# MoBA's q reaches its transposed layout by VectorE and DRAM in place of TensorE, and its scores are taken one weight chunk later

## The chip, the core and the metric

The kernel runs on one core of a Trainium2 chip. The metric is the device time of one execution in microseconds; the time before is the median of three runs, 388.99 us (388.95 to 389.02). One further execution was profiled: it took 388.81 us, and the span from its first to its last recorded instruction is 387.0 us.

## What is computed

Two layers of a decoder trunk, 256 tokens, model width 1024, all in float32. Each layer normalises x, multiplies it by one wide matrix (1024 x 5120), and splits the result into ten column groups of 512; three attention-like branches use them, and their gated outputs are multiplied by a second matrix (1536 x 1024) and added to x. Cut to what matters here:

```python
h = rms_norm(x, norm_g[l])
proj = h @ w_in[l]
q_a, k_a, v_a, q_h, f_h, i_h, q_m, z = jnp.split(proj, split_points, axis=-1)
qa = partial_rope(rms_norm(q_a.reshape(B, S, 8, 64), moba_q_norm[l]), positions)
ka = partial_rope(rms_norm(k_a.reshape(B, S, 8, 64), moba_k_norm[l]), positions)
o_a = moba_attention(qa, ka, va)                # 256 tokens are one block: causal softmax(qa ka^T / 8) va
o_h = hgrn2_chunkwise(q_h, f_h, i_h, lb_all[l]) # gated linear recurrence, 4 heads of 128
o_m = memory_attention(qm, km, vm)              # softmax over 256 memory tokens, 4 heads of 128
y = jnp.concatenate([o_a, o_h, o_m], axis=-1) * jax.nn.silu(z)
x = x + y @ w_out[l]
```

The change lies between q_a and the scores of `moba_attention`. With 256 tokens there is one block per head, so MoBA is plain causal attention over 8 heads of 64.

## The kernel before

**Weights.** All weights stream from DRAM in 120 chunks of 128 x 1024 (512 KB), 60 in each layer: 8 for the memory's keys and values, 40 for `w_in` (ten groups of 4), 12 for `w_out`. SyncE's queue loads a chunk into one of four buffers `wr`. ScalarE rounds it to the matmul's input type (`wh`, line 214), VectorE takes the rest (`wl = wr - wh`, line 228), and TensorE multiplies by high and low parts separately, three products for each. There are three buffers each of `wh` and `wl`; ScalarE and VectorE so work two to three chunks ahead of TensorE, and everything else that they do stands in their queues between these steps. Chunks are named below by their number in the layer: 16 to 19 are MoBA's k, 20 to 23 HGRN's input, 24 to 27 MoBA's q, 28 to 31 a gate (`zh`), 32 to 35 the memory's q (`qm`), 36 to 39 MoBA's v, 40 to 47 the two other gates, 48 to 59 `w_out`. In `group_b` (chunks 16 to 39) a chunk is 12 matmuls of 128 x 512, a group 48, and the accumulator of the first 128 tokens is complete three matmuls before the group's end.

**Order.** Branch work is written as Python generators. `slot()` and `step()` advance them between the matmuls of the chunks, and `yield n` lets n such steps pass. A scheduler then lays the instructions of each engine into one fixed order; the engines follow it without reordering and wait for each other by semaphores. `in_turn(...)` forces an order on one engine by hand (it adds no wait), `mm_row` keeps a matmul where the program has it. `order_of_attention` holds these hand-written lists for chunks 36 to 43: VectorE's and ScalarE's steps of the MoBA softmax between the weight steps.

**MoBA's q and k.** `g_qk` (line 976) takes a group's two accumulators `acc[t]`, t the half of the tokens. For each it squares and sums (lines 625, 626), takes the power -1/2 on GpSimd (`rqa`, line 982) and applies the rotary step on VectorE into `kr` (lines 985 to 992). The scores need q and k with the head dimension on the partitions. For k, `across` (line 88) does that: one VectorE transpose within 32 x 32 blocks (line 95), one DMA to DRAM (`there`, line 106), four DMAs back (line 111) into "strips", an order of columns that `strips()` describes. For q, eight TensorE transposes of 128 x 128 in two groups of four (line 1017) write PSUM, and two ScalarE copies (line 1018) make `qT`. q's norm is not applied to q but inside the softmax, as the factors `rq` and `nr` (lines 996, 998).

**Scores and softmax.** `g_moba` starts after chunk 32. The scores (lines 1113 and 1041, `sd<-kT,qT` and `acc<-kT,qT`) stand in one block of 16 matmuls; each float32 one shows as two records. VectorE masks them and takes row maxima (line 1033), `nba` (line 1056) is the negated maximum, ScalarE takes the exponentials (line 1062), VectorE divides (line 1070) and turns the probabilities by `across` through GpSimd's queue (`turned0`, `turned1`). HGRN's result `zh` and the memory branch's probabilities go through the same queue after them.

Of the kernel before, what the change touches and what calls it, by code (L numbers as in the profile page):

```python
# [28 lines left out]
EPS = 1e-6  # L29
# [16 lines left out]
def hymba_kernel(ctx: ExitStack, tc: tile.TileContext, x, mem, mem_t, positions, w_in, w_out, w_mem_kv,  # L46
# [38 lines left out]
        return sb.tile([128, n], F32, name=name, tag=name, bufs=2)  # L85


    def across(dst, src, n, stage=None, free=None, name=None, q=None, behind=None):
        q = q or nc.sync
        if stage is None:  # L90
            yield from room("blk")
            held["blk"] += 1
        tag = stage or "blk"
        blk = sb.tile([128, 4, n * 32], F32, name="blk", tag=tag, bufs=1)
        N["across", name] = nc.vector.transpose(blk.rearrange("p c (n i) -> p c n i", n=n),
                                                src.rearrange("p (n c i) -> p c n i", n=n, c=4))
        if free is not None:
            rel(free)
        if name is not None:
            done.add(name)  # L100
        yield 2
        while behind is not None and behind not in done:
            yield
        there = away.tile([4, 32, 4, n * 32], F32, name="there", tag="there", bufs=5)
        with tc.issue_after(T[behind].ins) if behind is not None else nullcontext():
            q.dma_start(there.rearrange("q j c r -> (q j) c r"), blk)
        if stage is None:
            rel("blk")
        yield 4
        for c in (0, 2, 1, 3):  # L110
            ins = q.dma_start(dst[c * 32:c * 32 + 32], there[:, :, c].rearrange("q j r -> j q r"))
# [163 lines left out]
    def mm(o, a, b, s, e):  # L275
        nc.tensor.matmul(o, lhsT=a, rhs=b, start=s, stop=e)  # L276


    def mm_row(o, a, b, s=True, e=True):
        tc.keep_in_program_order(nc.tensor.matmul(o, lhsT=a, rhs=b, start=s, stop=e))  # L280

    def group_b(th, tl):
        acc = [acc_tile() for _ in range(2)]
        for c in range(4):
            i = st["c"]
            for j in range(2):
                k = 2 * c + j
                wH, wL = whs[i][:, j * 512:(j + 1) * 512], wls[i][:, j * 512:(j + 1) * 512]
                for t in range(2):
                    ts = slice(t * 128, (t + 1) * 128)  # L290
                    mm(acc[t], th[:, k, ts], wH, k == 0, False)
# [511 lines left out]
    def g_hgrn(l):  # L803
# [8 lines left out]
        def carry(m, Tm, src, dst=None):  # L812
            (Qv, Kv), (Qo, Ko) = ([halves(a, m) for a in p] for p in (src, dst or src))
            n = 1024 // (2 * m)
            Tv = Tm.rearrange("p (n two) -> p n two", two=2)
            nc.vector.tensor_tensor(Qo[:, :, 1], Qv[:, :, 1], Tv[:, :, 0:1].to_broadcast([128, n, m]), op=OP.mult)
            nc.vector.tensor_tensor(Ko[:, :, 0], Kv[:, :, 0], Tv[:, :, 1:2].to_broadcast([128, n, m]), op=OP.mult)
# [103 lines left out]
        carry(64, T2, other)  # L921
        S2 = St.rearrange("p (a b) s -> p a b s", b=2)
        for q in range(0, 128, 32):
            nc.scalar.copy(St[q:q + 32, :, q:q + 32], hSd[q:q + 32])
        for m, o in ((32, 0), (64, 128)):
            for q in range(0, 128, 2 * m):
                for b in range(2):
                    p = q + b * m
                    nc.scalar.copy(S2[q:q + m, :, b, q + m:q + 2 * m],
                                   g[p:p + m, o:o + 4 * m].rearrange("p (a s) -> p a s", s=m))  # L930
        rel()
        Q4, K4 = (a.rearrange("p (h s) -> p h s", h=4) for a in other)
        yield 3
# [7 lines left out]
        nc.scalar.copy(xc, g)  # L941
        rel()
        yield 2
        while not {f"ih{l}", f"z{H_}{l}"} <= done:
            yield
        ih = T["ih"]
        po = []
# [25 lines left out]
    def g_qk(l, q, acc):  # L973
        ss = small("ssa", 16)
        ms = small("msa", 16)
        r = small("rka" if q else "rqa", 16)
        kr = sb.tile([128, 2, 512], F32, name="kr", tag="qk", bufs=1)
        for t in range(2):
            t8 = slice(t * 8, t * 8 + 8)
            sumsq(ss[:, t8], acc[t], 8)  # L980
            nc.vector.tensor_scalar(ms[:, t8], ss[:, t8], 1.0 / 64, EPS, op0=OP.mult, op1=OP.add)  # L981
            nc.gpsimd.tensor_tensor(r[:, t8], ms[:, t8], pw[:, :8], op=OP.pow)  # L982
            a3 = heads(acc[t], 8)
            k3 = heads(kr[:, t], 8)
            nc.vector.tensor_tensor(k3, a3, rtA[:, l, q, t][:, None, :].to_broadcast([128, 8, 64]), op=OP.mult)
# [6 lines left out]
            nc.vector.tensor_tensor(k3[:, :, 0:16], k3[:, :, 0:16], tm, op=OP.add)  # L992
            yield
        if q == 0:
            rq = small("rq", 16)
            nc.gpsimd.tensor_scalar(rq, r, 0.125, None, op0=OP.mult)
            nr = small("nr", 16)
            nc.gpsimd.tensor_scalar(nr, r, -0.125, None, op0=OP.mult)
# [8 lines left out]
        yield 2  # L1007
        tg = ("qT", "kT")[q]
        flat = kr.rearrange("p t s -> p (t s)")
        o = sb.tile([128, 1024], F32, name=tg, tag=(f"yl{M_}", f"yh{M_}")[q], bufs=1)  # L1010
        if q == 0:
            o = o.rearrange("p (h s) -> p h s", h=4)
            for t in range(2):
                yield from room("sd")
                pt = side_tile()
                for p in range(4):
                    nc.tensor.transpose(pt[:, p * 128:(p + 1) * 128], kr[:, t, p * 128:(p + 1) * 128], ident)  # L1017
                nc.scalar.copy(o[:, :, t * 128:(t + 1) * 128], heads(pt, 4))
                rel()
                yield  # L1020
# [16 lines left out]
    def second(u, ps):  # L1037
        qT, kT = T["qT"], T["kT"]
        for pi in range(2):
            for e in range(2):  # L1040
                mm_row(ps[e][:, pi * 256:(pi + 1) * 256].rearrange("p (t q i) -> p t q i", t=2, q=4),
                       qT[64 * e:64 * e + 64, 2 * u + pi, 128:256], strips(kT)[64 * e:64 * e + 64, 2 * u + pi])
        return ps

# [49 lines left out]
    def g_moba(l):  # L1094
# [20 lines left out]
        seconds = [second(0, first), second(1, [acc_tile() for _ in range(2)])]  # L1115
        yield
        for u in range(2):
            for p in (2 * u, 2 * u + 1):
# [127 lines left out]
    def order_of_attention(l):  # L1246
        c = 60 * l
        w = lambda k, i: (k, c + i)
        in_turn(("last mask", 0), ("nba", 0), ("first mask", 1), ("last mask", 1), ("nba", 1), w("wl", 36), ("ria", 0),
                *(("scale", 0, i) for i in range(5)), ("ss", "h", 0), *(("scale", 0, i) for i in range(5, 8)),  # L1250
                ("ss", "h", 1), w("wl", 37), ("across", f"turned0{l}"), ("ms", "hg"), ("ss", "qm", 0), w("wl", 38),
# [161 lines left out]
```

## Time and profile before

| | |
|---|---|
| median of three runs | 388.99 us |
| profiled execution | 388.81 us, span 387.0 us |
| granted TensorE clock | 1.000 |
| DMA, mean over the span | 218 GB/s |
| DMA, share of 16 engines: SyncE's queue, GpSimd's queue | 55.8%, 10.9% |

A row of the timeline or the chain is: start in us from the span's start, duration in us, engine (PE is TensorE, PEld its weight loads, DVE VectorE, ACT ScalarE, POOL GpSimd), source line, operation, out<-in, shape, count, and in brackets the engine's idle time before it with what ended it. Rows of one engine overlap a little, since an instruction's record runs on while the next has started. A row of a tile gives the minimum, median and maximum duration in ns. A DMA row on POOL shows the time of the issue; the landing is told apart.

### The profile page before, as it was taken

The page shows a single profiled execution, that of the slowest core. Times are in us where ns is not written, and L with a number is a line of the kernel's source. Part 1 is how long each engine was busy: PE and PEld are TensorE (multiplying, and loading weights), DVE is VectorE, ACT ScalarE, POOL GpSimd, SP SyncE. Part 2 cuts the span into 40 slices and gives each one's busy share as a digit, 9 for nine tenths or more (in the row PEclk, how much of TensorE's full clock was granted, in tenths as well). Part 3 has the DMA queues.
Part 4 walks back from the last instruction along what each step waited for, and adds up shares of the span by engine and source line. Part 5 has one row for each costly group of instructions (what it writes and reads, how often), then busy time and mean ns, then how long its engine had stood idle before and what let it go on. Part 6 is the DMA issues. An engine that isn't in the chain of part 4 may idle for free.

```text
span 387.0 us, 6782 instructions
## 1 busy us (share of the span) xinstructions
PE 381.9 (99%) x2455; PEld 319.7 (83%) x2455; DVE 320.4 (83%) x621; ACT 248.0 (64%) x414; POOL 86.8 (22%) x129
## 2 busy tenths in 40 slices
PE   8999999999999999999999999999999999999996
PEld 5888887788888888788888888888888888887885
DVE  4789799999669999967577689899698699798663
ACT  5998755567769749754375756445765985785540
POOL 3004400734203523400000040014062063232000
PEclk9999999999999999999999999999999999999999
DMA  8986594539635889985454568735766189999502
GB/s 260 420 313 202 175 329 166 164 112 285 209 105 188 269 257 341 322 255 178 161 204 164 174 208 237 252 110 179 255 190 197 54 275 271 346 300 272 188 36 108
DMA packets 26241, 84.48 MB, mean 218 GB/s; under 512 B 3552, under 2 KB 5984, under 8 KB 26208
## 3 DMA queue, kind: packets, MB, share of 16 engines
q1 hardware_dynamic: 22304, 71.31, 55.8%
q0 software_dynamic: 3616, 12.59, 10.9%
q8 instruction: 19, 0.31, 0.3%
q10 hardware_dynamic: 288, 0.15, 0.1%
q14 instruction: 14, 0.11, 0.1%
HBM read 74.60 MB, written 9.44 MB: 217 GB/s over the span
## 4 chain that ended last, share of the span: by engine, by line
PE 86%; DVE 6%; POOL 2%; issue 2%; DMA 2%; ACT 1%; SPq 0%; DVEq 0%; ACTq 0%
PE acc L276 58%; PE acc L1285 17%; PE sd L276 6%; PE sd L280 3%; DVE wl L228 2%; DMA wr<-in_w_mem_kv_dram 2%; POOL mk L605 1%; PE sd L489 1%; DVE as L360 0%; PE sd L1145 0%; PE sd L1017 0%; PE acc L280 0%; POOL rk L651 0%; DVE ssa L626 0%; DVE rt L547 0%
## 5 line engine op out<-in xcount | busy, mean ns | idle before, releaser
L214 ACT CAST wh<-wr 128x1024 fp32r<-128x1024 f32 x96 | 100.8, 1051 | 62.2 <-PE acc L276 43.1
L228 DVE TENSOR_TENSOR wl<-wr,wh 128x1024 fp32r<-128x1024 f32 x96 | 117.3, 1223 | 25.7 <-ACT wh L214 23.6
L276 PE MATMUL acc<-wh,hT 128*128 128x512 f32 x384 | 123.1, 394 | 0.1
L276 PEld LDWEIGHTS acc<-wh,hT 128*128 128x128 f32 x384 | 71.5, 188 | 15.2 <-issue 0.7
L276 PE MATMUL acc<-wl,hT 128*128 128x512 f32 x192 | 75.6, 394 | 0.0
L276 PE MATMUL acc<-hT,wh 128*128 128x512 f32 x256 | 64.0, 392 | 0.0
L276 PEld LDWEIGHTS acc<-hT,wh 128*128 128x128 f32 x256 | 46.4, 189 | 8.9 <-ACT kn L639 0.4
L276 PEld LDWEIGHTS acc<-wl,hT 128*128 128x128 f32 x192 | 36.1, 188 | 7.3
L1285 PE MATMUL acc<-wh,yl 128*128 128x512 f32 (+1 forms) x96 | 37.2, 387 | 0.0
L1285 PE MATMUL acc<-wl,yh 128*128 128x512 f32 (+1 forms) x96 | 37.2, 387 | 0.0
L232 DVE SCALAR_TENSOR_TENSOR wl<-wr,gT,wh 128x1024 fp32r<-128x1024 f32 (+1 forms) x29 | 31.2, 1098 | 6.7 <-ACT wh L218 6.6
L276 PEld LDWEIGHTS acc<-hT,wl 128*128 128x128 f32 x256 | 34.8, 190 | 2.2
L218 ACT ACTIVATE wh<-wr,gT 128x1024 fp32r<-128x1024 f32 (+1 forms) x29 | 28.4, 1002 | 11.8 <-PE acc L276 4.0
L276 PE MATMUL acc<-hT,wl 128*128 128x256 f32 x256 | 35.7, 282 | 0.0
L1285 PE MATMUL acc<-wh,yh 128*128 128x512 f32 (+1 forms) x96 | 33.1, 392 | 0.0
L276 PE MATMUL acc<-wh,mTh 128*128 128x512 f32 x64 | 25.6, 403 | 0.4 <-DVE ti L601 0.2
L982 POOL TENSOR_TENSOR rka<-msa,pw 128x8 f32<-128x8 f32 x4 | 12.1, 3027 | 58.2 <-DVE msa L981 58.2
L276 PE MATMUL acc<-wh,mTl 128*128 128x512 f32 x64 | 24.8, 390 | 0.0
L1062 ACT ACTIVATE P<-P,nba,rq 128x128 f32<-128x128 f32 (+1 forms) x32 | 17.1, 538 | 7.0 <-DVE nba L1056 7.0
L1285 PEld LDWEIGHTS acc<-wh,yh 128*128 128x128 f32 x96 | 18.0, 188 | 4.1 <-issue 0.7
L1285 PEld LDWEIGHTS acc<-wh,yl 128*128 128x128 f32 x96 | 18.0, 188 | 3.7
L1285 PEld LDWEIGHTS acc<-wl,yh 128*128 128x128 f32 x96 | 18.0, 188 | 3.5
(222 smaller groups left out, 591.8 us busy)
## 6 DMA issues: line engine op xcount, KB each, us to landing
wr<-in_w_in_dram SPq DMA_DIRECT2D x80, 512.0 KB, 4.2
wr<-in_w_out_dram SPq DMA_DIRECT2D x24, 512.0 KB, 6.2
wr<-in_w_mem_kv_dram SPq DMA_DIRECT2D x15, 512.0 KB, 4.1
there<-blk POOLq DMA_DIRECT2D x4, 768.0 KB, 6.3
PT<-there POOLq DMA_DIRECT2D x16, 192.0 KB, 5.4
there<-blk POOLq DMA_DIRECT2D x6, 512.0 KB, 5.5
there<-blk SPq DMA_DIRECT2D x4, 512.0 KB, 2.9
P<-there POOLq DMA_DIRECT2D x16, 128.0 KB, 6.8
```

Source lines behind the costliest of these rows:

```text
L214: N["wh", i] = nc.scalar.copy(whs[i], raws[i])
L218: N["wh", i] = nc.scalar.activation(whs[i][:, sl], raws[i][:, sl], AF.Copy, scale=gT[:, g:g + 1])
L228: N["wl", i] = nc.vector.tensor_tensor(wls[i], raws[i], whs[i].bitcast(F32), op=OP.subtract)
L232: ins = nc.vector.scalar_tensor_tensor(wls[i][:, sl], in0=raws[i][:, sl], scalar=gT[:, g:g + 1], in1=whs[i][:, sl].bitcast(F32), op0=OP.mu ...
L276: nc.tensor.matmul(o, lhsT=a, rhs=b, start=s, stop=e)
L280: tc.keep_in_program_order(nc.tensor.matmul(o, lhsT=a, rhs=b, start=s, stop=e))
L489: ins = nc.tensor.transpose(pt[:, j * 256 + t * 128:j * 256 + (t + 1) * 128], xn[t][:, k * 128:(k + 1) * 128], ident)
L605: nc.gpsimd.tensor_scalar(mk[:, j], xf[:, q], float(least), None, op0=OP.is_ge)
L982: nc.gpsimd.tensor_tensor(r[:, t8], ms[:, t8], pw[:, :8], op=OP.pow)
L1062: N["exp", u, c] = nc.scalar.activation(P[:, i, kc[t]], P[:, i, kc[t]], AF.Exp, bias=nb[:, c:c + 1], scale=rq[:, r:r + 1], accum_out=sm[:, ...
L1285: ins = nc.tensor.matmul(a, lhsT=y, rhs=wt[:, cs], start=n == (0 if to is None else nk - 2) and j == 0, stop=n == nk - 1 and j == 2)
```

## The change

`g_qk` no longer transposes q on TensorE. For q it now does the two rotary steps first (without the yields between them), spawns `across` on GpSimd's queue, and only then the sums of squares and the powers (`spread`). When the last of the four DMAs back is issued (`q moved`), the powers may follow on GpSimd, and two ScalarE copies bring the strips into `qTs`, laid out as `qT` was.

```diff
-    def across(dst, src, n, stage=None, free=None, name=None, q=None, behind=None):
+    def across(dst, src, n, stage=None, free=None, name=None, q=None, behind=None, pace=(2, 4)):
...
-        yield 2
+        yield pace[0]
...
-        yield 4
+        yield pace[1]
...
+        o = sb.tile([128, 1024], F32, name=tg, tag=(f"yl{M_}", f"yh{M_}")[q], bufs=1)
         if q == 0:
+            spawn(across(o.rearrange("p (q r) -> p q r", q=4), flat, 8, name=f"q{l}", q=nc.gpsimd, pace=(1, 1)))
+            while f"q{l}" not in done:
+                yield
+            for t in range(2):
+                spread(t)
...
         if q == 0:
-            o = o.rearrange("p (h s) -> p h s", h=4)
+            while f"q{l}moved" not in done:
+                yield
+            N["q moved"] = T[f"q{l}moved"]
+            in_turn("q moved", ("pow", 0))
+            qT = sb.tile([128, 4, 256], F32, name="qTs", tag=f"yl{A_}", bufs=1)
             for t in range(2):
-                yield from room("sd")
-                pt = side_tile()
-                for p in range(4):
-                    nc.tensor.transpose(pt[:, p * 128:(p + 1) * 128], kr[:, t, p * 128:(p + 1) * 128], ident)
-                nc.scalar.copy(o[:, :, t * 128:(t + 1) * 128], heads(pt, 4))
-                rel()
-                yield
+                N["qT", t] = nc.scalar.copy(strip_of(qT, t), strips(o)[:, :, t])
+            o = qT
```

HGRN's output step now also waits (in the generators, not on an engine) until the scores have been written into the program (`seen`). `order_of_attention` gets three lists more: on VectorE the weight steps 28 and 29, then q's rotary steps and its transpose, then weight step 30, HGRN's `carry` and q's sums; on ScalarE the ten copies `hST` of HGRN behind weight step 29; on TensorE the last score ahead of chunk 34's first matmul.

```diff
+        in_turn(w("wl", 28), w("wl", 29), ("rope", 0), ("rope", 1), ("across", f"q{l}"), w("wl", 30), "carry Q", "carry K",
...
+        in_turn("score", ("mm", c + 34, 0, 0))
```

**TensorE, layer 0, from HGRN's last carry block to the memory's q.** `ident,kr` are q's transposes, `kT,qT` the scores, `ident,qm` the memory's transposes. Before (rows numbered as they stand in the built program; those left out are matmuls of the weight chunks):

```order
238 L276 MATMUL sd<-hQb,hKb 128x128 x4
...
256 L1017 MATMUL sd<-ident,kr 128x128 x4
...
262 L1017 MATMUL sd<-ident,kr 128x128 x4
...
276 L280 MATMUL sd<-kT,qT 128x128 x8
277 L280 MATMUL sd<-kT,qT 128x256 x4
278 L280 MATMUL acc<-kT,qT 128x256 x4
...
323 L1145 MATMUL sd<-ident,qm 128x128 x4
...
332 L1145 MATMUL sd<-ident,qm 128x128 x4
```

After (chunk matmuls now carry two line numbers, so that the row numbers do not compare):

```order
306 L276 MATMUL sd<-hQb,hKb 128x128 x4
...
340 L280 MATMUL sd<-kT,qTs 128x128 x8
341 L280 MATMUL sd<-kT,qTs 128x256 x4
342 L280 MATMUL acc<-kT,qTs 128x256 x4
...
387 L1160 MATMUL sd<-ident,qm 128x128 x8
```

Counted with their multiples, 204 chunk matmuls of `group_b` stood ahead of the scores in either layer before, and 217 do now: 13 more. The eight transposes `ident,kr` are gone. The second four of the memory's transposes (`ident,qm`) had ten chunk matmuls between them and the first four and now follow these at once, behind 254 chunk matmuls, where the first four stood before.

**VectorE, layer 0, around q's rotary step.** Before (`kr<-acc,rtA` and the rows up to `kr<-kr,tm` are one half of the tokens each):

```order
138 L817 TENSOR_TENSOR hKb<-hKb,hT_1107 128x8x64
139 L228 TENSOR_TENSOR wl<-wr,wh 128x1024
140 L626 TENSOR_REDUCE ssa<-sq 128x8
141 L985 TENSOR_TENSOR kr<-acc,rtA 128x512
...
147 L992 TENSOR_TENSOR kr<-kr,tm 128x8x16
148 L985 TENSOR_TENSOR kr<-acc,rtA 128x512
...
152 L228 TENSOR_TENSOR wl<-wr,wh 128x1024
153 L992 TENSOR_TENSOR kr<-kr,tm 128x8x16
```

After:

```order
140 L994 TENSOR_TENSOR kr<-acc,rtA 128x512
141 L996 TENSOR_TENSOR tm<-acc,rtB 128x8x8
142 L998 TENSOR_TENSOR tm<-acc,rtB 128x8x8
143 L1002 TENSOR_TENSOR kr<-kr,tm 128x8x16 x2
144 L95 STREAM_TRANSPOSE blk<-kr 128x1024
145 L228 TENSOR_TENSOR wl<-wr,wh 128x1024
146 L818 TENSOR_TENSOR hQb<-hQb,hT_1107 128x8x64
147 L819 TENSOR_TENSOR hKb<-hKb,hT_1107 128x8x64
148 L628 TENSOR_REDUCE ssa<-sq 128x8 x2
```

q's rotary steps moved ahead of HGRN's carry (`hQb`, `hKb`), of one weight step and of the sums, and the transpose of q follows them.

**ScalarE, layer 0, ahead of the exponentials.** Before:

```order
75 L941 COPY hX<-sd 128x512
76 L214 CAST wh<-wr 128x1024 x2
77 L1018 COPY qT<-sd 128x4x128 x2
78 L757 ACT_TABLE_LOAD
79 L757 ACTIVATE sg<-acc 128x512
80 L214 CAST wh<-wr 128x1024
81 L757 ACTIVATE sg<-acc 128x512
82 L214 CAST wh<-wr 128x1024
83 L1062 ACT_TABLE_LOAD
84 L1062 ACTIVATE P,sma_1434<-P,nba_1433,rq 128x128 x4
```

After:

```order
74 L943 COPY hX<-sd 128x512
75 L759 ACT_TABLE_LOAD
76 L759 ACTIVATE sg<-acc 128x512
77 L214 CAST wh<-wr 128x1024
78 L759 ACTIVATE sg<-acc 128x512
79 L1033 COPY qTs<-qT 128x4x128 x2
80 L214 CAST wh<-wr 128x1024
81 L1076 ACT_TABLE_LOAD
82 L1076 ACTIVATE P,sma_1457<-P,nba_1456,rq 128x128 x4
```

The two copies of q moved from ahead of the gate's sigmoids (`sg`) to behind them, directly ahead of the `wh` step of chunk 35 (row 80). On GpSimd the write and the four reads of q now stand ahead of q's two powers, where nothing of the kind stood. SyncE's order is unchanged.

More of the change, by code (lines that the diff above doesn't have):

```diff
@@ L279, in mm_row @@
     def mm_row(o, a, b, s=True, e=True):
-        tc.keep_in_program_order(nc.tensor.matmul(o, lhsT=a, rhs=b, start=s, stop=e))
+        ins = nc.tensor.matmul(o, lhsT=a, rhs=b, start=s, stop=e)
+        tc.keep_in_program_order(ins)
+        return ins
     def group_b(th, tl):
@@ L290, in group_b @@
                     ts = slice(t * 128, (t + 1) * 128)
-                    mm(acc[t], th[:, k, ts], wH, k == 0, False)
+                    N["mm", i, j, t] = nc.tensor.matmul(acc[t], lhsT=th[:, k, ts], rhs=wH, start=k == 0, stop=False)
                     mm(acc[t], th[:, k, ts], wL, False, False)
@@ L815, in carry @@
             Tv = Tm.rearrange("p (n two) -> p n two", two=2)
-            nc.vector.tensor_tensor(Qo[:, :, 1], Qv[:, :, 1], Tv[:, :, 0:1].to_broadcast([128, n, m]), op=OP.mult)
-            nc.vector.tensor_tensor(Ko[:, :, 0], Kv[:, :, 0], Tv[:, :, 1:2].to_broadcast([128, n, m]), op=OP.mult)
+            N["carry Q"] = nc.vector.tensor_tensor(Qo[:, :, 1], Qv[:, :, 1], Tv[:, :, 0:1].to_broadcast([128, n, m]), op=OP.mult)
+            N["carry K"] = nc.vector.tensor_tensor(Ko[:, :, 0], Kv[:, :, 0], Tv[:, :, 1:2].to_broadcast([128, n, m]), op=OP.mult)
             if dst is not None:
@@ L923, in g_hgrn @@
         for q in range(0, 128, 32):
-            nc.scalar.copy(St[q:q + 32, :, q:q + 32], hSd[q:q + 32])
+            N["hST", q // 32] = nc.scalar.copy(St[q:q + 32, :, q:q + 32], hSd[q:q + 32])
         for m, o in ((32, 0), (64, 128)):
@@ L928, in g_hgrn @@
                     p = q + b * m
-                    nc.scalar.copy(S2[q:q + m, :, b, q + m:q + 2 * m],
-                                   g[p:p + m, o:o + 4 * m].rearrange("p (a s) -> p a s", s=m))
+                    N["hST", 4 + (4 if o else q // 32) + b] = nc.scalar.copy(
+                        S2[q:q + m, :, b, q + m:q + 2 * m], g[p:p + m, o:o + 4 * m].rearrange("p (a s) -> p a s", s=m))
         rel()
@@ L943, in g_hgrn @@
         yield 2
-        while not {f"ih{l}", f"z{H_}{l}"} <= done:
+        while not {f"ih{l}", f"z{H_}{l}", f"seen{l}"} <= done:
             yield
@@ L977, in g_qk, with spread @@
         kr = sb.tile([128, 2, 512], F32, name="kr", tag="qk", bufs=1)
+        flat = kr.rearrange("p t s -> p (t s)")
+        tg = ("qT", "kT")[q]
+        def spread(t):
+            t8 = slice(t * 8, t * 8 + 8)
+            sumsq(ss[:, t8], acc[t], 8, "qk", t)
+            nc.vector.tensor_scalar(ms[:, t8], ss[:, t8], 1.0 / 64, EPS, op0=OP.mult, op1=OP.add)
+            N["pow", t] = nc.gpsimd.tensor_tensor(r[:, t8], ms[:, t8], pw[:, :8], op=OP.pow)
         for t in range(2):
[L979 to L982, printed above, removed]
+            if q:
+                spread(t)
             a3 = heads(acc[t], 8)
@@ L1040, in second @@
             for e in range(2):
-                mm_row(ps[e][:, pi * 256:(pi + 1) * 256].rearrange("p (t q i) -> p t q i", t=2, q=4),
+                N["score"] = mm_row(ps[e][:, pi * 256:(pi + 1) * 256].rearrange("p (t q i) -> p t q i", t=2, q=4),
                        qT[64 * e:64 * e + 64, 2 * u + pi, 128:256], strips(kT)[64 * e:64 * e + 64, 2 * u + pi])
@@ L1115, in g_moba @@
         seconds = [second(0, first), second(1, [acc_tile() for _ in range(2)])]
+        done.add(f"seen{l}")
         yield
@@ L1248, in order_of_attention @@
         w = lambda k, i: (k, c + i)
+        in_turn(w("wl", 28), w("wl", 29), ("rope", 0), ("rope", 1), ("across", f"q{l}"), w("wl", 30), "carry Q", "carry K",
+                ("ss", "qk", 0), ("ss", "qk", 1), w("wl", 31))
+        for i in range(10):
+            in_turn(w("wh", 28), w("wh", 29), ("hST", i))
+        in_turn("score", ("mm", c + 34, 0, 0))
         in_turn(("last mask", 0), ("nba", 0), ("first mask", 1), ("last mask", 1), ("nba", 1), w("wl", 36), ("ria", 0),
```

15 lines of the change are left out of this document (8 added, 7 removed).

## The prediction

> **What bounds the kernel now.** First the page's parts 1 and 4: busy time and share of the span, then the shares of the chain that ended last.
>
> ```profile
> PE 381.9 (99%) x2455; PEld 319.7 (83%) x2455; DVE 320.4 (83%) x621; ACT 248.0 (64%) x414; POOL 86.8 (22%) x129
> ...
> PE 86%; DVE 6%; POOL 2%; issue 2%; DMA 2%; ACT 1%; SPq 0%; DVEq 0%; ACTq 0%
> ```
>
> TensorE is the bound. Then the chain of waits in the two stretches that change, 84 to 124 us (layer 0) and 270 to 300 us (layer 1); columns are start, duration, engine and line, count.
>
> ```profile
> 85.41 6.58 PE acc L276 x28
> ...
> 98.33 0.44 PE sd L1017 x4
> ...
> 100.17 0.44 PE sd L1017 x4
> ...
> 104.72 1.96 PE sd L280 x24
> 106.68 0.86 PE acc L280 x8
> ...
> 121.85 0.44 PE sd L1145 x4
> ```
>
> ```profile
> 274.63 5.90 PE acc L276 x25
> ...
> 287.33 0.44 PE sd L1017 x4
> ...
> 290.09 0.44 PE sd L1017 x4
> ...
> 293.30 1.96 PE sd L280 x24
> ```
>
> Each piece begins where the one before it ends: TensorE never stands there. So what leaves its queue moves all that follows forward, as long as what TensorE needs next is ready that much earlier. 0.2% of the time, 0.78 us, is about what a measurement of this kernel can tell from no change; the question is whether more than that survives.
>
> **Term A, the transposes.** The tile `kr` gives the duration of one (minimum, median, maximum in ns), and of VectorE's block transpose, which q now gets as k did.
>
> ```profile
> L1017 PE MATMUL sd<-ident,kr x16: 270/272/273, 98.2 to 290.3; 128*128 128x128 f32 x16
> ...
> L95 DVE STREAM_TRANSPOSE blk<-kr x2: 1243/1244/1246, 85.6 to 269.9; 128x1024 f32<-128x1024 f32 x2
> ```
>
> Two prices offer themselves: 16 x 272 ns = 4.35 us by duration, or 4 x 0.44 = 1.75 us by the four pieces of the chain. Matmuls overlap, so the record of one runs on while the next has begun; what TensorE's queue loses is the chain's piece. I take 1.75, 0.87 a layer. The Trainium skill ("TensorE: Matmul & The Clock Gate", Part 4: PE-mode transpose) gives about 275 ns for a 128x128 transpose in one kernel's context; the trace agrees with the duration, 272 ns, but a sum by it would be an estimate of 4.4 us and a time near 384.6, which the chain's spacing contradicts.
>
> **Term B, q's new path.** TensorE reaches the scores 13 matmuls later, at 6.58 / 28 = 0.235 each, 3.05 us, and 0.87 earlier for the transposes: 104.72 + 3.05 - 0.87 = 106.9 in layer 0, 293.30 + 3.05 - 0.87 = 295.5 in layer 1. Is q there by then? VectorE's rows around the rotary step in layer 0:
>
> ```profile
> 86.76 1.19 DVE L228 TENSOR_TENSOR wl<-wr,wh 128x1024 fp32r<-128x1024 f32 x1
> ...
> 90.92 0.68 DVE L985 TENSOR_TENSOR kr<-acc,rtA 128x512 f32<-128x512 f32 x1
> ...
> 91.78 0.16 DVE L981 TENSOR_SCALAR msa<-ssa 128x8 f32<-128x8 f32 x1
> ```
>
> The order puts weight steps 28 (at 86.76) and 29 ahead of q; at about 1.15 each the second ends at 89.1. q's first accumulator is complete 13 matmuls into the piece at 85.41, at 88.5, so VectorE decides. Two halves at 0.86 (90.92 to 91.78, the first three of their steps), 0.2 each for the last step, and 1.24 for the transpose: GpSimd can issue the write at 92.5. In layer 1 the accumulator is complete 10 matmuls after 274.63, at 277.0, and the same 3.4 lead to 280.4. From there the nearest rows are HGRN's result, through the same function and queue with the same shapes; first GpSimd's rows (write, four reads; then the first probabilities' write and reads), then from the tile `zh` the reads' landing (us) and ScalarE's copy of such strips, and from the tile `there` the time of an issue:
>
> ```profile
> 132.68 0.64 POOL L106 DMA_DIRECT2D there<-blk  x1
> 137.96 2.22 POOL L111 DMA_DIRECT2D zh<-there  x4 [4.64 <-DMA there<-blk]
> 140.26 0.56 POOL L106 DMA_DIRECT2D there<-blk  x1
> 149.49 2.24 POOL L111 DMA_DIRECT2D PT<-there  x4 [8.67 <-DMA there<-blk]
> ```
>
> ```profile
> L129 ACT CAST yh<-zh x4: 608/616/623, 154.2 to 343.3; 128x512 fp32r<-128x512 f32 x4
> ...
> DMA to landing us min/median/max: 3.9/5.0/5.8
> ```
>
> ```profile
> L111 POOL DMA_DIRECT2D PT<-there x16: 550/554/614, 128.3 to 338.2; - x16
> ```
>
> Write to first read 5.3, three more issues 1.65, landing 5.0 to 5.8: 12.0 to 12.8 us. q is in SBUF at 104.4 to 105.2 in layer 0 and 292.3 to 293.1 in layer 1; two copies of 0.6, overlapping a little, end 1.1 later, 105.5 to 106.3 and 293.4 to 294.2. Against 106.9 and 295.5 that leaves 0.6 to 1.4 and 1.3 to 2.1 us: the scores don't wait, and B costs nothing. That cover is thin in layer 0; the price without it is the third rival.
>
> **Term C, the softmax starts later, and its end has little slack.** In layer 0, VectorE's weight step 35, the first mask, the negated maximum of the first half and weight step 38, then the first matmul that needs that step; the same in layer 1.
>
> ```profile
> 105.85 1.22 DVE L228 TENSOR_TENSOR wl<-wr,wh 128x1024 fp32r<-128x1024 f32 x1
> 106.98 0.28 DVE L1033 CUSTOM_DVE_ANT_0 P<-sd,cm 128x128 f32<-128x128 f32 x1
> ...
> 110.39 0.16 DVE L1056 TENSOR_TENSOR nba<-mxa,nr 128x8 f32<-128x8 f32 x1
> ...
> 122.79 1.23 DVE L228 TENSOR_TENSOR wl<-wr,wh 128x1024 fp32r<-128x1024 f32 x1
> ```
>
> ```profile
> 125.36 0.40 PE L276 MATMUL acc<-wl,hT 128*128 128x512 f32 x1
> ```
>
> ```profile
> 294.41 1.23 DVE L228 TENSOR_TENSOR wl<-wr,wh 128x1024 fp32r<-128x1024 f32 x1 [1.38 <-ACT wh L214]
> ...
> 311.23 1.24 DVE L228 TENSOR_TENSOR wl<-wr,wh 128x1024 fp32r<-128x1024 f32 x1
> ```
>
> ```profile
> 313.92 0.40 PE L276 MATMUL acc<-wl,hT 128*128 128x512 f32 x1
> ```
>
> Weight step 38 ends at 124.02 and is used at 125.36: 1.34 us of slack; in layer 1 at 312.47 for 313.92: 1.45. Between the masks and that step VectorE and ScalarE run the same instructions as before, in one chain (masks, `nba`, exponentials, division, transpose), so I let it move as a whole. Two things gate the masks. The first eight scores are done some 1.0 us into their block (half of 1.96): 107.9 and 296.5. And ScalarE's copies of q stand ahead of its step 35:
>
> ```profile
> 104.76 1.05 ACT L214 CAST wh<-wr 128x1024 fp32r<-128x1024 f32 x1 [0.18 <-PE acc L276]
> ```
>
> That cast begins only after the copies, so 105.5 to 106.3 plus 0.95 for it and 1.14 for VectorE's step gives 107.6 to 108.4 (295.5 to 296.3 in layer 1). The later gate decides: masks at 107.9 to 108.4, 0.9 to 1.4 after 106.98, and in layer 1 0.95 after 294.41 + 1.14 = 295.55. `nba` now waits for one mask fewer, which gives some 0.3 back (13 masks fill the 3.41 us from 106.98 to 110.39, 0.26 each, the later and wider ones more). The chain is late by 0.6 to 1.1, taken as 0.85, in layer 0 and by 0.65 to 0.85, taken as 0.75, in layer 1, while TensorE comes 0.87 earlier. TensorE then waits at chunk 38 for 0.87 + 0.85 - 1.34 = 0.4 us in layer 0, and 0.87 + 0.75 - 1.45 = 0.2 in layer 1. Net: -0.5 and -0.7, **-1.2 us together**. If the chain stretches a little (weight DMAs, q's extra steps on VectorE) up to 0.3 more a layer is lost: -0.55; if it absorbs part of the shift: -1.55.
>
> **Costed at nothing, with their cover.** The second four of `ident,qm` stand ten matmuls earlier and need ScalarE's second copy of `qm`:
>
> ```profile
> 119.94 0.60 ACT L1131 COPY qm<-acc 128x512 f32<-128x512 f32 x1
> ```
>
> It ended at 120.54; 0.85 later is 121.4, and TensorE is at them at 121.85 - 0.87 + 0.44 = 121.4. A wait here would be taken out of the one at chunk 38, so it isn't added. q's two powers now stand on GpSimd behind five issues, the first 5.3 us apart:
>
> ```profile
> L982 POOL TENSOR_TENSOR rqa<-msa,pw x4: 1635/2646/5076, 92.0 to 286.0; 128x8 f32<-128x8 f32 x4
> ```
>
> ```profile
> 97.73 0.86 POOL L996 TENSOR_SCALAR rq<-rqa 128x16 f32<-128x16 f32 x1
> 98.57 0.26 POOL L998 TENSOR_SCALAR nr<-rqa 128x16 f32<-128x16 f32 x1
> ```
>
> The reads are issued by 92.5 + 5.3 + 2.2 = 100.0; two powers at 2.65 and 1.1 for `rq` and `nr` end at 106.4, at 5.08 each at 111.3. `nba` needs `nr` at 110.39 + 0.85 = 111.2: hidden, and at the far end 0.1 us late. On SyncE's queue nothing moves, but q's megabyte (write and reads, 512 KB each) falls into a full stretch (busy of five engines, clock, DMA share, GB/s):
>
> ```profile
> 87.00:104.00 17.00, 17.00 (x84) 14.21 (x84) 13.35 (x22) 12.61 (x19) 6.39 (x4) 1.00 0.90 278
> ```
>
> At 278 GB/s a megabyte is 3.8 us of DMA. Weight chunks are fetched ahead, and in this stretch ScalarE waited for one only once:
>
> ```profile
> 92.13 1.05 ACT L214 CAST wh<-wr 128x1024 fp32r<-128x1024 f32 x1 [0.93 <-DMA wr<-in_w_in_dram]
> ```
>
> I cost the megabyte at nothing for the weights and carry it as a risk for q itself.
>
> **The rivals.** *Full gain* (0.12): the chain absorbs the shift, all of A stays, -1.75: 387.2. For it: a shift of 0.47 and 0.58 would be free (slack less 0.87), and the bounds begin at 0.6. Against: no step between the masks and weight step 38 is taken away. *All given back* (0.15): the chain is late by 1.3 to 1.4, TensorE waits 0.9 a layer at chunk 38, and the time is 389.0 (388.4 to 389.7). For it: the q-gate alone reaches 1.4. *q late, slower than before* (0.21): q's write or reads take longer than `zh`'s, as the write at 140.26 did (9.2 us to its first read, 3.9 more than `zh`'s), because 0.90 of the DMA engines' time is taken. If q lands d later than I said, masks follow the q-gate, and the net is d - 0.7 in layer 0 and d - 1.4 in layer 1 (the q-gate's middle, 108.0 and 295.9, shifts the chain by 0.7 and 0.05 after the 0.3 of `nba`; less the slacks of 1.34 and 1.45). It decides from d = 1.0, where the two sum to nothing; d = 1.5 gives +0.9 and 389.9, d = 3.9 gives +5.7 and 394.7. Against: k's writes and reads, on SyncE's queue, meet the same weights in both layers, and the tile `kT` gives for their reads
>
> ```profile
> DMA to landing us min/median/max: 3.5/4.8/6.3
> ```
>
> hardly more than `zh`'s.
>
> *GpSimd's issues blocked by VectorE* (0.02): if each of the five issues waited for a VectorE step of up to 1.24 us to end, d = 6.2, +10.3, about 399. The row of `there` speaks against it: 16 issues took 550 to 614 ns with VectorE busy beside them. The Trainium skill names it ("SBUF — State Buffer", SBUF: two separate sides, the "DVE blocks DMA" trap): a copy engine step of VectorE in float32 locks GpSimd out of writing descriptors, 620 ns becoming some 3100; no issue in this trace shows that. The rest (0.02) is for what I don't see.
>
> **How the numbers follow.** The profiled execution took 388.81, 0.18 under the median; the change of -1.2 is taken off the median of 388.99: **387.8**. The forecast has 0.48; its own range is -1.55 to -0.55, 387.4 to 388.4, most of it (0.37) past -0.78. Faster: 0.37 + 0.12 = 0.49. Same: 0.11 + 0.15 = 0.26. Slower: 0.21 + 0.02 + 0.02 = 0.25. The range runs from 387.0, the full gain and a little for the measurement, to 390.5, q late by 1.8; beyond lie the later part of the third rival and the two small ones, under 0.2.
>
> **What would show it.** In the changed profile: no L1017, and the first score at 106.9 and 295.5 without idle time of PE before it; q's last read landing at 104.4 to 105.2 and 292.3 to 293.1; first masks at 107.9 to 108.4 and 296.5; idle time of PE of 0.4 and 0.2 at the first `acc<-wl,hT` of chunk 38. Idle time before `sd<-kT,qTs`, or ScalarE idle ahead of the copies to `qTs` for long, shows the third rival; issues far over 0.6 us on GpSimd the fourth; none before chunk 38, the first. The forecast is wrong if TensorE stands elsewhere in chunks 28 to 39, for weights above all.

## The result and the profile after

The changed kernel is slower: 392.69 us median (390.57 to 393.24, six runs) against 389.00 (388.47 to 389.22), ratio 1.009 with a 95% interval of 1.0074 to 1.0106. The profiled execution took 392.44 us, span 390.7; its mean granted TensorE clock is 0.994. The runs lie 2.7 us apart, those of the kernel before 0.75. One run in the whole record counts as slow (395.52 us, of the changed kernel run again) and is left out of the figures below.

First the page: busy time, and the shares of the chain that ended last.

```profile
PE 381.4 (98%) x2439; PEld 319.3 (82%) x2439; DVE 322.9 (83%) x623; ACT 247.4 (63%) x414; POOL 84.6 (22%) x139
...
PE 79%; DVE 8%; DMA 5%; ACT 3%; issue 2%; POOL 1%; SPq 0%; ACTq 0%; DVEq 0%
```

TensorE's busy time fell by only 0.5 us, though the transposes are gone: in layer 0 the scores' block took 4.5 us (109.86 to 114.35) where it took 2.8, at the lowered clock shown below. 5% of the chain is now DMA, where 2% was. The chain of waits of layer 0 shows which:

```profile
89.05 0.60 DVE kr L994
...
91.21 1.26 DVE blk L95
...
92.78 7.02 DMA there<-blk
...
100.10 1.67 POOL qT L111 x3
101.77 7.32 DMA qT<-there
...
109.71 0.61 ACT qTs L1033
110.32 0.96 ACT wh L214
...
111.30 1.22 DVE wl L228
```

From 89 to 129 us the chain runs through q's trip and then through VectorE and ScalarE, and through nothing of TensorE's. Rotary step and transpose are where they were forecast (89.1, 92.5). The write then takes 7.02 us to land, 7.3 to the first read instead of 5.3, and the last read 7.32 instead of 5.0 to 5.8: q is in SBUF at 109.1 instead of 104.4 to 105.2. TensorE's timeline shows what that costs at the scores, VectorE's how it reaches weight step 38 (first mask, `nba`, the weight step), and TensorE's again the first use of that step:

```profile
109.86 3.70 PE L280 MATMUL sd<-kT,qTs 64*128 64x128 f32 x24 [3.10 <-ACT qTs L1033]
```

```profile
112.44 0.28 DVE L1047 CUSTOM_DVE_ANT_0 P<-sd,cm 128x128 f32<-128x128 f32 x1
...
115.70 0.17 DVE L1070 TENSOR_TENSOR nba<-mxa,nr 128x8 f32<-128x8 f32 x1
...
128.21 1.21 DVE L228 TENSOR_TENSOR wl<-wr,wh 128x1024 fp32r<-128x1024 f32 x1
```

```profile
129.48 0.50 PE L276 MATMUL acc<-wl,hT 128*128 128x512 f32 x1
```

The masks are 5.5 us later than before, weight step 38 is 5.4 later, and the matmul that needs it starts at 129.48 where it started at 125.36: layer 0 loses 4.1 us. No wait stands ahead of that matmul in this profile, because TensorE was late by itself: the granted clock (third number from the end) was 0.50 behind the stand at the scores. In a second profile of the same kernel, the run of the changed kernel again, it was 1.00:

```profile
110.00:112.00 2.00, 2.00 (x18) 2.00 (x20) 0.70 (x1) 1.98 (x3) 0.00 (x0) 0.50 0.00 0
```

```profile
110.00:112.00 2.00, 2.00 (x27) 1.96 (x24) 1.15 (x2) 1.98 (x2) 0.00 (x0) 1.00 0.00 0
```

```profile
125.19 0.66 PE L1160 MATMUL sd<-ident,qm 128*128 128x128 f32 x4 [1.07 <-ACT qm L1146]
...
129.03 0.50 PE L276 MATMUL acc<-wl,hT 128*128 128x512 f32 x1 [0.40 <-DVE wl L228]
```

There the scores' block took 2.9 us and TensorE waited for the late chain instead, at the memory's second transposes and at chunk 38. From k's write on SyncE's queue to that matmul it needed 42.3 us, the first profile 42.6, the kernel before 38.5. So the late masks set the loss, and the clock hardly changed it. Layer 1 (the scores, then the same matmul; first mask and weight step 38):

```profile
299.40 2.03 PE L280 MATMUL sd<-kT,qTs 64*128 64x128 f32 x24
...
317.43 0.50 PE L276 MATMUL acc<-wl,hT 128*128 128x512 f32 x1 [0.16 <-DVE wl L228]
```

```profile
300.60 0.29 DVE L1047 CUSTOM_DVE_ANT_0 P<-sd,cm 128x128 f32<-128x128 f32 x1 [0.93 <-PE sd L280]
...
316.13 1.24 DVE L228 TENSOR_TENSOR wl<-wr,wh 128x1024 fp32r<-128x1024 f32 x1
```

There the matmul starts 3.5 us later than before (313.92), so layer 1 gives 0.6 of the 4.1 back. No wait stands ahead of its scores, and of the 0.2 us forecast at chunk 38, 0.16 is there. The whole loss is in layer 0, and it begins with q's DMAs.

Why those are late in layer 0 can be read from the DMA view cut into slices of 1 us. Its queue rows are packets, MB and the time that the packets took as a share of 16 engines; q1 is SyncE's queue (weights and k), q0 GpSimd's. The slices from 92, 94 and 95 us:

```profile
q1 hardware_dynamic: 311, 0.33, 109.0%
```

```profile
q1 hardware_dynamic: 75, 0.25, 94.7%
```

```profile
q1 hardware_dynamic: 139, 0.20, 67.1%
q0 software_dynamic: 25, 0.10, 35.4%
```

q's write is issued at 92.78, but none of its packets shows before 95.4 (in slices of 0.2 us). Until then the engines carry what SyncE had issued just before, between 87.3 and 92.0: three weight chunks and k's four reads, 2 MB (the next chunk follows at 93.6). In layer 1 the write is issued at 285.47, 4.9 us after SyncE issued k's last read and 3.8 after its last weight chunk, and its first packet shows 1.2 us later.

### The profile page after: what moved, and what is told of

Read it like the earlier page. It is cut to its first block, busy times and chain, and to the rows that moved or that the text cites. A ratio compares the mean times of both kernels' runs of the same rounds, so it can differ in the third digit from the quotient of the medians.

```text
span 390.7 us, 6777 instructions
## 1 busy us (share of the span) xinstructions
PE 381.4 (98%) x2439; PEld 319.3 (82%) x2439; DVE 322.9 (83%) x623; ACT 247.4 (63%) x414; POOL 84.6 (22%) x139
## 4 chain that ended last, share of the span: by engine, by line
PE 79%; DVE 8%; DMA 5%; ACT 3%; issue 2%; POOL 1%; SPq 0%; ACTq 0%; DVEq 0%
PE acc L276 48%; PE acc L1305 17%; PE acc L293 7%; PE sd L276 4%; PE sd L280 2%; ACT P L1076 2%; DMA qT<-there 2%; DMA there<-blk 2%; DMA wr<-in_w_mem_kv_dram 2%; DVE P L1047 2%; DVE wl L228 2%; DVE P L1084 1%; PE sd L491 1%; DVE blk L95 1%; ACT wh L214 1%
## 5 line engine op out<-in xcount | busy, mean ns | idle before, releaser
L276 PE MATMUL acc<-wh,hT 128*128 128x512 f32 x192 | 75.3, 392 | 0.0
L293 PE MATMUL acc<-wh,hT 128*128 128x512 f32 x192 | 70.4, 393 | 0.0
L987 POOL TENSOR_TENSOR rka<-msa,pw 128x8 f32<-128x8 f32 x4 | 9.9, 2475 | 58.2 <-DVE msa L986 58.2
```

Of the source, the lines that this page charges most:

```text
L293: N["mm", i, j, t] = nc.tensor.matmul(acc[t], lhsT=th[:, k, ts], rhs=wH, start=k == 0, stop=False)
L987: N["pow", t] = nc.gpsimd.tensor_tensor(r[:, t8], ms[:, t8], pw[:, :8], op=OP.pow)
```

## The experiments

The theory: terms A and C are as forecast, and only q's trip in layer 0 is wrong; its packets stand behind those that SyncE's queue has just issued. The rivals: the transposes were worth something else; the new order of VectorE and ScalarE costs by itself; GpSimd's queue is slow by itself, or held up by VectorE. Kernels that ran together share the runs of the kernel before (medians 388.58 to 388.66). Profiles begin up to 2.3 us apart on their axes (k's write on SyncE's queue starts at 85.9 to 88.2 us), so that times are compared against a mark inside each.

**Transposes left out.**

```diff
-                pt = side_tile()
-                for p in range(4):
-                    nc.tensor.transpose(pt[:, p * 128:(p + 1) * 128], kr[:, t, p * 128:(p + 1) * 128], ident)
-                nc.scalar.copy(o[:, :, t * 128:(t + 1) * 128], heads(pt, 4))
-                rel()
+                nc.scalar.copy(o[:, :, t * 128:(t + 1) * 128], heads(kr[:, t], 4))
```

> The kernel before, with q's 16 TensorE transposes left out: ScalarE copies the rotated q into its place without turning it, so the scores are of the wrong elements; the order of every engine else stays. It prices term A alone. By the chain's 0.44 us for four: 1.75 us less, 387.2 (387.0 to 387.6), no wait at chunk 38 since the masks stand behind weight step 35 and don't move. Rival, by the duration of 272 ns each: 4.35 us less, 384.6. Second rival: the slack of weight step 38 is smaller than read, and 0.5 us or more is given back: 387.8 or over.

386.65 us against 388.64, ratio 0.9945 (0.9925 to 0.9965): 1.4 to 2.9 us, which holds 1.75 and excludes 4.35. The median lies 0.35 us under the range set down. Between k's write on SyncE's queue and the first score there are 16.84 us (87.99 to 104.83) where there were 17.78 (86.87 to 104.65): 0.94 in layer 0 (1.00 in layer 1 by the same marks) against the 0.87 taken. The chain's spacing is the price of a transpose in TensorE's queue, and its duration is not.

**k in place of q.**

```diff
-                N["qT", t] = nc.scalar.copy(strip_of(qT, t), strips(o)[:, :, t])
+                N["qT", t] = nc.scalar.copy(strip_of(qT, t), strips(T["kT"])[:, :, t])
```

Further lists in the manner of `in_turn` hold the scores, the copies and the memory's transposes where the changed kernel has them.

> The changed kernel, but the two copies read k's strips (ready long before) in place of q's, so that the scores are of k with k; q is still turned, written and read back, and every engine's order is that of the changed kernel. It takes away the wait for q alone. Theory (q's late landing is the whole of the loss): no idle time ahead of the scores, masks at about 107.9 and, in layer 1, some 1.0 later against TensorE's scores than before, and the forecast of my terms A and C, 387.8 (387.4 to 388.4). Rival (the new order of VectorE and ScalarE, or the traffic beside the weights, costs by itself): 390 or over.

388.21 us, ratio 0.999 (0.9973 to 1.0008); the profiled execution took 387.80. VectorE's and TensorE's rows in layer 0:

```profile
107.79 0.29 DVE L1047 CUSTOM_DVE_ANT_0 P<-sd,cm 128x128 f32<-128x128 f32 x1 [1.52 <-PE sd L280]
...
123.57 1.22 DVE L228 TENSOR_TENSOR wl<-wr,wh 128x1024 fp32r<-128x1024 f32 x1
```

```profile
124.84 0.50 PE L276 MATMUL acc<-wl,hT 128*128 128x512 f32 x1 [0.39 <-DVE wl L228]
...
312.80 0.50 PE L276 MATMUL acc<-wl,hT 128*128 128x512 f32 x1 [0.16 <-DVE wl L228]
```

Masks at 107.8 (forecast 107.9), waits of 0.39 and 0.16 at chunk 38 (0.4 and 0.2), layer 0 gaining 125.36 - 124.84 = 0.5 (0.5), both layers 313.92 - 312.80 = 1.1 (1.2); this profile's axis begins 0.1 us earlier by k's write, which makes it 0.4 and 1.0. Terms A and C hold step by step, and the rival of a cost in the new order falls: the loss is the wait for q. The medians are less clear than the trace (interval from -1.0 to +0.3 us).

**Half the weights around q's trip.**

```diff
-            raws[i] = sb.tile([128, 1024], F32, name="wr", tag="wr", bufs=RAW_BUFS)
-            load(raws[i], ap)
+            if 30 <= i <= 40 and i % 2 == 0:
+                raws[i] = raws[i - 1]
+            else:
+                raws[i] = sb.tile([128, 1024], F32, name="wr", tag="wr", bufs=RAW_BUFS)
+                load(raws[i], ap)
```

> The changed kernel with half the weight bytes around q's trip in layer 0: the even chunks 30 to 40 take the data of the chunk ahead of them and aren't loaded, so part of the products are wrong; every engine but SyncE keeps its order. Theory (q's write and reads share full DMA engines with weight chunks): write to first read falls from 7.3 us to 4 to 5.5, landing from 7.3 to 4 to 5.5, q in SBUF by 105, no or little idle time at the scores, 387.5 to 388.5, and the spread of the runs shrinks. Rival (GpSimd's queue is slow by itself, or VectorE holds up its issues): q lands at 108 to 110 as before, 392 to 393.

391.46 us, ratio 1.0062 (1.0039 to 1.0086): the expectation missed. The reads landed sooner (median 3.5 us), q was in at 105.2 and no wait stood ahead of the scores. But the write took longer than in the changed kernel, 8.2 us to the first read, its first packet 4.6 us after the issue: SyncE had issued chunks 1.8 and 0.3 us ahead of it (90.06 and 91.54). The time can't be used: TensorE waited 1.8 us for ScalarE elsewhere, and 1.1 for the second copy of `qm`.

**No weights while q moves**, and the same with an earlier chunk (28 for chunks 29 to 38) as the source:

```diff
+            raws[i] = st["r30"] if 31 <= i <= 38 else sb.tile([128, 1024], F32, name="wr", tag="wr", bufs=RAW_BUFS)
+            31 <= i <= 38 or load(raws[i], ap); st["r30"] = raws[i] if i == 30 else st.get("r30")
```

> The changed kernel with no weight chunk loaded while q moves in layer 0: chunks 31 to 38 take the data of chunk 30 and aren't loaded (their products are wrong), three later chunks are fetched ahead of q's write; every engine but SyncE keeps its order. Theory (q's packets wait behind packets of SyncE's queue on full DMA engines): write to first read 3 to 5 us, landing 3.5 to 4.5, q in SBUF by 102, TensorE doesn't stand at the scores, 387.3 to 388.5. Second theory (behind k's reads alone): the write is still late, 6.5 us or more, but the reads land in 4, q by 105. Rival (GpSimd's queue is slow by itself): 7 us each and q at 107 or later, 391 or over.

> As the run without weights, but chunks 29 to 38 of layer 0 take the data of chunk 28, so that the three later chunks are fetched well before q's write and only k's trip stands ahead of it on SyncE's queue; q stays on GpSimd's queue and VectorE's order is that of the changed kernel. Theory (q's packets start when the packets that SyncE issued before them are through): the first packet 1.2 us after the issue or soon after, as in layer 1, write to first read 3 to 4.5, landing 2.8 to 4, q in SBUF 8.5 to 10.5 us after its write was issued. Rival (GpSimd is held up by VectorE, whose steps are unchanged): the first packet again 2 to 2.6 us or more after the issue, write to first read over 5.5. The total is of little use, since the products of ten chunks are wrong and the stream behind them shifts; 387.2 to 389 by the theory.

388.90 us, ratio 1.0014 (0.9999 to 1.0029), and 388.62, ratio 0.999 (0.9974 to 1.0006). In both, with the buffers free, SyncE issued three later chunks directly ahead of q's write (from 92.85 and from 91.02), which the second kernel was meant to avoid. GpSimd's rows of the first, and its queues in the slices from 97 and 99 us:

```profile
94.11 0.80 POOL L106 DMA_DIRECT2D there<-blk  x1 [12.04 <-DVE blk L95]
102.28 2.22 POOL L111 DMA_DIRECT2D qT<-there  x4 [7.38 <-DMA there<-blk]
```

```profile
q1 hardware_dynamic: 70, 0.28, 94.6%
```

```profile
q1 hardware_dynamic: 70, 0.24, 59.7%
q0 software_dynamic: 40, 0.16, 39.8%
```

The first packet came 5.2 us after the issue, in the second kernel 5.0, later than with all weights. The reads, with nothing issued beside them, landed in 2.8 to 2.9. By the numbers set down, "write late, reads quick" in the first kernel was the second theory's (behind k's reads alone), and the second kernel's late packet was the rival's (GpSimd held up by VectorE). Neither follows: k's reads and VectorE's steps stand there in every run, and what grew is the number of chunks directly ahead.

**SyncE still.** Four buffers are held, so that nothing but k's trip is on SyncE's queue:

```diff
+            raws[i] = st["r", (i - 26) % 4] if 30 <= i <= 45 else sb.tile([128, 1024], F32, name="wr", tag="wr", bufs=RAW_BUFS)
+            30 <= i <= 45 or load(raws[i], ap); st["r", (i - 26) % 4] = raws[i]
```

> As the run before it, but now no weight chunk at all is issued between chunk 29's load, ahead of k's write, and the use of chunk 42: chunks 30 to 45 of layer 0 take the data of chunks 26 to 29 in turn (their products are wrong). In the two runs without weights three chunks were issued directly ahead of q's write after all, and its first packet came 5 us late. Here only k's write and reads stand ahead of it. Theory (q's packets start behind what SyncE has just issued): first packet 1 to 1.6 us after the issue, as in layer 1, write to first read 3 to 4.5 us, landing 2.6 to 3.5; the masks stand by the scores. Rival (GpSimd held up by VectorE's steps, which are the same): first packet 2 to 2.6 us after the issue or later, write to first read 5.5 or more.

387.67 us against 388.64, ratio 0.9976 (0.9953 to 0.9999). GpSimd's rows, and the DMA issues from 88 to 108 us (KB each, median us to landing):

```profile
92.34 0.80 POOL L106 DMA_DIRECT2D there<-blk  x1 [12.05 <-DVE blk L95]
95.79 2.22 POOL L111 DMA_DIRECT2D qT<-there  x4 [2.65 <-DMA there<-blk]
```

```profile
kT<-there SPq DMA_DIRECT2D x4, 128.0 KB, 2.6
there<-blk POOLq DMA_DIRECT2D x1, 512.0 KB, 3.1
qT<-there POOLq DMA_DIRECT2D x4, 128.0 KB, 2.8
```

First packet 1.4 us after the issue, 3.45 to the first read, landing 2.8. VectorE's steps beside it are the same as in the changed kernel, and q is on GpSimd's queue: that queue isn't slow by itself, and VectorE doesn't hold it up. This settles what the runs ahead left open. With q in time over its own path, TensorE waited 0.38 and 0.17 us at chunk 38, as forecast. The Trainium skill ("DMA: Bandwidth & Descriptors", Anatomy of one DMA) fits one such transfer by 2.0 us plus bytes over 436 GB/s, an estimate of 3.2 for 512 KB; the row's 3.1 agrees, and the 7.0 of the changed kernel shows how far a busy stretch is from it. The Trainium skill ("SBUF — State Buffer", SBUF: two separate sides) has VectorE's float32 copies hold up GpSimd's descriptors. VectorE ran no such copy between q's write and its landing in this run, so that rule is not tried here; GpSimd's issues took 0.55 to 0.80 us in every profile.

**The change in layer 1 alone**, and there with the scores seven matmuls earlier. The old code and order stay for layer 0 by a condition on `l`; then in the second kernel

```diff
-            in_turn("score", ("mm", c + 34, 0, 0))
+            for j, t in ((1, 0), (1, 1)):
+                in_turn("score", ("mm", c + 33, j, t))
```

> Layer 0 as in the kernel before (TensorE transposes, scores at the old place), layer 1 as in the changed one; computes the whole reference. Theory (layer 1 gains what the prediction said, the loss is all in layer 0): 0.5 to 0.8 less than before, 388.2 to 388.5. Rival (layer 1 only looked well because layer 0 had run late, and q is late there too when it hasn't): 389.5 or over.

> As the run with the change in layer 1 alone, but the scores of layer 1 stand seven matmuls earlier (six later than in the kernel before) and the memory's second four transposes ten matmuls behind the first again. Computes the whole reference. By that run's trace q's copies ended 2.5 us ahead of the scores in layer 1, so 1.6 of it can be taken: the masks move back by 1.6, TensorE doesn't wait at chunk 38, and all of 0.87 is kept: 387.6 to 388.0 against 388.64 before (ratio 0.997 to 0.998). Rival (q lands later in most runs than in the one profiled): as the other run or worse, 388.1 or over.

388.12 us, ratio 0.9983 (0.9965 to 1.0), and 387.91, ratio 0.998 (0.9967 to 0.9994). The first is 0.5 us faster where 0.5 to 0.8 was expected, with an interval that reaches no change. Its trace is clearer: from k's write to chunk 38 in layer 1 it needs 42.08 us where the kernel before needs 42.77. Layer 1 keeps its gain when layer 0 isn't late. The second is 0.7 faster, its profile has no wait at chunk 38, but 0.2 us between the two isn't resolved.

**q on SyncE's queue.**

```diff
-            spawn(across(o.rearrange("p (q r) -> p q r", q=4), flat, 8, name=f"q{l}", q=nc.gpsimd, pace=(1, 1)))
+            spawn(across(o.rearrange("p (q r) -> p q r", q=4), flat, 8, name=f"q{l}", q=nc.sync, pace=(1, 1)))
-            in_turn("q moved", ("pow", 0))
```

The same further lists hold the order of the other engines.

> The changed kernel with q's write and four reads on SyncE's queue, where k's are, in place of GpSimd's; one weight load stands between write and reads, the others behind the reads; TensorE's, VectorE's and ScalarE's order is held as it was. Computes the whole reference. Theory (contention, not the queue): the write is as late as before or a little less, 5 to 7 us, but the reads meet fewer weights, 4 to 5; q in SBUF at 103 to 105.5, TensorE stands at most 0.5 at the scores, 387.7 to 389. Rival (weights held behind q's reads starve ScalarE): over 389.5, with ScalarE waiting for DMA in chunks 34 to 36.

387.97 us, ratio 0.9982 (0.9964 to 1.0). SyncE's rows, and ScalarE's wait for q:

```profile
92.15 0.34 SPq L106 DMA_DIRECT2D there<-blk  x1
93.26 0.35 SPq L178 DMA_DIRECT2D wr<-in_w_in_dram  x1
98.24 1.74 SPq L111 DMA_DIRECT2D qT<-there  x4
100.08 7.45 SPq L178 DMA_DIRECT2D wr<-in_w_in_dram  x5
```

```profile
103.83 1.14 ACT L1033 COPY qTs<-qT 128x512 f32<-128x512 f32 x2 [0.96 <-DMA qT<-there]
```

The write still waits out what was issued before it (6.1 us to the first read), but while SyncE waits for it, it issues no further weights, so the reads land in 2.5 to 4.2 (median 3.4) and q is in at 103.8. The scores don't wait, TensorE waits 0.38 and 0.17 us at chunk 38 (forecast 0.4 and 0.2), and ScalarE doesn't starve.

**The copies of q behind chunk 35's step.**

```diff
+        in_turn(w("wh", 35), ("qT", 0), ("qT", 1))
```

> The changed kernel with the two copies of q behind ScalarE's step of chunk 35 in place of ahead of it; all else as in the changed one but for one matmul by which the scores stand earlier. Computes the whole reference. Theory: q lands as late as before, TensorE stands at the scores as before (some 3 us), but the masks follow the scores and not weight step 35: some 1.0 to 1.3 of the 5.5 us by which they were late comes back, 391.2 to 391.8; layer 1 stays. Rival (the masks were bound by the scores anyway): 392.3 or over.

390.37 us (387.88 to 393.25), ratio 1.004 (1.0011 to 1.0069), below the range set down. In the profiled execution q came sooner, and TensorE stood 1.0 us at the scores instead of 3.1, so that the time doesn't price the copies' place. Its trace does: the first mask follows the first score by 110.10 - 108.91 = 1.2 us, where it was 112.44 - 109.86 = 2.6 (and 111.99 - 109.40 = 2.6 in the second profile of the changed kernel, at clock 1.00). When q is late, the copies ahead of ScalarE's step 35 cost another 1.4.

**q on SyncE's queue and the scores seven matmuls earlier in both layers; and the changed kernel again beside it.**

```diff
-        in_turn("score", ("mm", c + 34, 0, 0))
+        in_turn("score", ("mm", c + 33, 1, 0)); in_turn("score", ("mm", c + 33, 1, 1)); in_turn(("sgz", 1), ("qT", 0), ("qT", 1))
```

> The run with q on SyncE's queue, with the scores seven matmuls earlier in both layers (six later than in the kernel before) and the memory's second four transposes ten matmuls behind the first again. Computes the whole reference. In that run q's copies ended 1.5 us ahead of TensorE's scores in layer 0 and more in layer 1, and TensorE waited 0.4 and 0.2 for weight step 38. Theory (term C is a pure delay of one chain): the masks come back by 1.0 to 1.6, no wait at chunk 38, term A is kept almost whole, 1.3 to 1.75 under the kernel before (ratio 0.9955 to 0.9967). Rival (q lands as late as the scores in most runs, so the wait only moves to the scores): no better than the other run, 0.6 under the kernel before.

> The changed kernel unaltered, beside the run with q on SyncE's queue and the kernel before on the same chip, and a second trace of it. Theory (its time is set by when q's packets get through): 2.5 to 4.5 over the kernel before, runs spread over 2 us or more, and in the trace the wait at the scores is as long as q's write and reads are late against 12.8 us. Rival (a fixed cost of the new order): the same excess in every run.

386.73 us against 388.60, ratio 0.995 (0.993 to 0.9969): 1.2 to 2.7 us faster, the version that beats both. There is no wait at the scores or at chunk 38, so term A is kept. (`sgz` names the gate's sigmoids; the pin holds the copies where they were. The memory's second four transposes stand ten matmuls behind the first again.) The changed kernel took 392.15 (389.47 to 393.95, six runs), ratio 1.008 (1.0048 to 1.0112), and its trace shows the same wait:

```profile
109.40 2.10 PE L280 MATMUL sd<-kT,qTs 64*128 64x128 f32 x24 [2.78 <-DMA wr<-in_w_in_dram]
```

The releaser named there is a weight load, but ScalarE's copies of q ended the wait; they started at 108.73 after 5.74 us of waiting for `qT<-there`. Its runs spread over 4.5 us, those of the kernel before beside it over 1.9, which fits the theory; but the 35 runs of the kernel before beside the run with no weights spread over 2.7, so spread alone proves little.

## Why the prediction was wrong

- **Term A** (1.75 us) was right to 0.2 us: 0.94 and 1.00 by the marks of the two layers with the transposes left out.
- **Term C** was right to 0.1 us in both layers, by the run with k in place of q, and in layer 1 of the changed kernel itself (-0.6 for -0.7).
- **Term B failed, in layer 0.** The step is "Write to first read 5.3, three more issues 1.65, landing 5.0 to 5.8: 12.0 to 12.8 us". It took 16.3 (92.78 to 109.1): 7.3 to the first read, 1.7 for the issues, 7.3 to land. In layer 1 it took 10.8, and there q's arrival came out right by luck: by k's write the issue was 0.9 us later than forecast, behind weight step 29, and the trip was 1.2 to 2.0 shorter. I took the duration from `zh`'s trip because function, queue and shapes were the same, and because both stretches have full engines; but ahead of `zh`'s write at 132.68 SyncE had issued one chunk in 5.5 us, and ahead of q's it had issued three, and k's four reads. The order in front of the prediction shows q's rotary step moved up, and with it the write moved to within 1.2 us of k's last read and 1.6 us of a weight chunk.
- **"SyncE's order is unchanged", so the megabyte costs nothing for the weights**: true, and it was the wrong question. The weights were in time; it was q that stood behind them.
- **The third rival** (0.21) is what happened, by its mechanism and its sign: d = 4.3 in layer 0. Its formula, d - 0.7 = 3.6, was 0.5 short of the 4.1 measured, for `nba` gave 0.15 and not 0.3 back and the masks stood 0.15 later than d says; by the prediction's own terms it is 0.7 - 1.34 = -0.64, so 3.7. It priced both layers alike, where layer 1 has d = 0. Against it I had held that `zh`'s and k's reads landed soon; that spoke for reads, and said nothing of what stands ahead of the write. Its example of a late write, at 140.26, moves 768 KB by its row of the DMA issues, half as much again as q's.
- The fourth rival (VectorE blocks GpSimd's issues) is excluded by the run with SyncE still, for the steps that VectorE runs here.

## What to carry to other kernels

A transfer's time is not a property of its size and queue: before moving one, see what the other queues issue in the two or so microseconds directly ahead of it, and take the duration from a place with the same issues ahead, not the same busy share. A step that frees the bounding engine but adds a wait on DMA needs a margin as wide as that DMA's spread, and where it has none, the order of issues (here: q's reads ahead of later weights on one queue) may supply it. The run with q on SyncE's queue changed order and queue at once; that GpSimd's queue was quick with SyncE still speaks for the order, but no run tried the order alone.

## What the runs showed of the hardware

- The first packet of q's write on GpSimd's queue came the later, the more weight chunks SyncE had issued in the 1.9 us ahead of it. With none it came after 1.2 to 1.4 us (layer 1, and SyncE still), with one after 2.1 to 2.6 (four profiles of layer 0), with two after 4.6 (half the weights), with three after 5.0 and 5.2 (the two runs without weights). The bytes issued in the 5.5 us ahead don't give this order: the changed kernel and the run with half the weights both had three chunks and k's reads there. The Trainium skill ("DMA: Bandwidth & Descriptors", Queues, rings and completion order) has each engine take turns between queues packet by packet. Once q's packets come, both queues do show side by side (the slice from 99 us above); why they begin so late that sentence does not say.
- Full engines alone don't explain it. In the second run without weights q's packets were missing from 92.5 to 97.5 us, while from 94 to 98 the 16 engines were 0.67 busy on average (the second number from the end):

```profile
94.00:98.00 4.00, 4.00 (x22) 3.38 (x21) 4.00 (x6) 2.72 (x3) 0.00 (x0) 1.00 0.67 225
```

  Why earlier packets of another queue hold later ones up at that share stays open.
- Behind the stand of 3.1 us the granted TensorE clock was 0.50 from 110 to 112 us; behind one of 2.8 us, in the second profile of the same kernel, it stayed at 1.00. What decides between the two stays open.
